# Dense products bank by bank, and neighbourhood scores with 128 rows throughout

## The chip, the cores and the metric

One core of one Trainium2 chip runs the whole program. The metric is the device time of one launch in microseconds (us), and lower is better. Five engines work side by side and wait for one another through semaphores: the matrix engine (PE in the profile, with its weight loads shown apart as PEld), the vector engine (DVE), the scalar engine (ACT), GpSimd (POOL) and the engine that issues most DMA transfers (SP). Matmuls read their operands from on-chip memory (SBUF) and write sums into eight banks of another memory (PSUM); a bank holds 512 columns of float32.

## What is computed

Two layers of a trunk over 512 latent tokens on a grid of 8 rows by 64 columns, and 256 context tokens ahead of them, 1024 channels wide. Each layer normalises and modulates the tokens, projects them once into four token mixers, weighs each mixer's output by a sigmoid gate, projects the sum, adds it to the residual, and ends with a squared-ReLU MLP:

```python
h = modulate(x, norm1, shift, scale)                # RMSNorm, adaLN
A, B, C, D = pool_mix, latent attention, neighbourhood attention, recurrence (all from h @ w_in)
proj = einsum('blnw,nwd->blnd', stack(A, B, C, D), w_br)
x += gate * (sum(sigmoid(gate_cols) * proj) @ w_o)
x += gate2 * (square(relu(modulate(x, norm2, ...) @ w1)) @ w2)
```

Context tokens read context tokens alone. In the neighbourhood attention a latent query reads the keys of an 8 x 16 window of the grid, with a bias by relative position, and all context keys; a context query reads the context keys. There are 4 heads of 64 channels. The second layer makes no output for the context tokens, so queries, gates and the MLP have 768 tokens in the first layer and 512 in the second; keys, values and forget gates have 768 in both.

## The kernel before

**Two parts of every operand.** Operands of the large products are split into a high part, rounded to the type float32r, and a low part, the rest. A product is three matmuls: high x high, high weight x low input, low weight x high input. All sum into the same bank.

**Dense products.** Channels stand on partitions, tokens along the columns. A unit of weights is 128 input rows x 8 k-tiles x 128 outputs (1024 input channels), loaded by SP, copied into its high part by the scalar engine (`unit`, line 69) and subtracted to its low part by the vector engine (line 70), one unit ahead of its use. `dense` (line 106) runs over the k-tiles; for each it calls `dense_step` (line 84), which goes through its targets. A target is a stretch of up to 512 tokens in one bank: 768 tokens have two targets, of 512 and 256 columns. `dense_step` issues the first two matmuls of each target (lines 88 and 89) and then, again for each target, the third (line 91). The room is a tile of two banks where the phase is "wide" (first layer, `p_big`, two such tiles) and a one-bank tile for each target otherwise. `dense_pair` runs two units together, one part of the tokens before the next; `dense_part` runs one part of the tokens alone. Both have their own loops.

**The merge.** `merge_steps` (line 1000) is a generator: for each output tile it makes a gate product of 8 k-tiles with a loop of its own, and yields after every second k-tile; then comes the product of the branch's output (2 k-tiles) and the sum. While a mixer runs, it calls `fill(n)`, which advances the generator of an earlier branch by n pieces. So pieces of gate products stand between the small matmuls of a mixer whose next operands come from other engines.

**Neighbourhood attention.** `na_att` runs over steps: a window of 128 queries (16 grid columns) and a head, 16 per layer, and in the first layer 128 context queries and a head, 8 in all. A step's scores are made by `products` (line 846). The keys of a head stand in 128 rows, the high part in the 64 rows where the head's channels are, the low part in the other 64. The query's high part `nqh` is copied into both halves (lines 853, 854), so that one 128-row matmul gives high query x both parts of the key (line 857). The query's low part `nql` fills only the head's 64 rows (line 855), and a second matmul of those 64 rows adds low query x high key (line 858). A window has two outputs of 256 columns in one bank, its local keys and the context keys, so four matmuls in turn; a context step has one output, so two. The softmax follows on the vector and scalar engines (lines 867 to 874), then transposes (line 705) and products with the values (line 890). Scores are one step ahead of their transposes.

**What sets the order.** The program is written in the order of the loops, and a planner arranges each engine's instructions from it ahead of the run, by priority and by when operands come free. On the chip each engine works through its list in that fixed order.

Of the kernel before, what the change touches and what calls it, by code (L numbers as in the profile page):

```python
# [8 lines left out]
F32 = mybir.dt.float32  # L9
# [26 lines left out]
# columns of the per-layer vectors  # L36
# [3 lines left out]
# channel-major units of the input projection  # L40
U_Z, U_G, U_Q, U_P, U_QA, U_CKV, U_NQ, U_NK, U_GATE = 0, 4, 6, 8, 10, 12, 13, 15, 17
# token-major groups
# [8 lines left out]
class K:  # L51
# [3 lines left out]
    # ---------------------------------------------------------------- weights  # L55
# [18 lines left out]
    def queue(self, specs):  # L74
        """Units are loaded and split a few ahead of the products that use them."""
        self.specs.extend(specs)
# [6 lines left out]
    # ---------------------------------------------------------------- dense products  # L83
    def dense_step(self, targets, w, kt, rhs, start, stop):
        """out += w[:, kt]^T @ rhs[:, kt, t0:t0+n], for each target (t0, n, out)."""
        mm = self.nc.tensor.matmul
        for t0, n, out in targets:
            mm(out, w.hi[:, kt], rhs.hi[:, kt, t0:t0 + n], start=start, stop=False)  # L88
            mm(out, w.hi[:, kt], rhs.lo[:, kt, t0:t0 + n], start=False, stop=False)  # L89
        for t0, n, out in targets:  # L90
            self.last_mm = mm(out, w.lo[:, kt], rhs.hi[:, kt, t0:t0 + n], start=False, stop=stop).ins  # L91

    def outputs(self, n):
        """Room for the products of the first n tokens: the targets of matmuls, and pieces (t0, n, ap) to read."""
        if self.wide:
            out = self.p_big.tile([P, 1024], F32, name="big")
            return [(a, min(n, a + 512) - a, out[:, a:min(n, a + 512)]) for a in range(0, n, 512)], [(0, n, out[:, :n])]
        return self.narrow_outputs(n)
# [7 lines left out]
    def dense(self, w, kts, rhs, n, narrow=False):  # L106
        targets, pieces = self.narrow_outputs(n) if narrow else self.outputs(n)
        for kt in range(kts):
            self.dense_step(targets, w, kt, rhs, kt == 0, kt == kts - 1)
        return pieces  # L110

    def dense_part(self, w, kts, rhs, t0, n, big):
        """The product for the tokens t0..t0+n alone."""
# [8 lines left out]
    def dense_pair(self, ws, kts, rhs, n, parts, between=None):  # L122
        """Two units at once, a part of the tokens (t0, n) before the next; between() is called early in the first."""
# [11 lines left out]
    def tokmajor(self, out, units, rhs, toks):  # L135
        """out[tokens, ncols] = rhs[:, :, tokens]^T @ w, w in units of some k-tiles each."""
# [17 lines left out]
    def lnexp(self):  # L154
        """Ln and Exp from one table set, for what follows on the engine"""
        self.tc.keep_in_program_order(self.nc.scalar.preload_act_table_set("natural_log_exp_and_others"))

    def rstd(self, out, ms, scale=1.0):
        """(ms * scale + eps) ** -0.5"""
# [3 lines left out]
    def rstd_rows(self, out, sqs, ones, n, hl, scale=1.0):  # L163
        """out[:, :n] = (scale * sum over partitions of sq + eps) ** -0.5 on every partition; the two parts of sq go to hl"""
# [13 lines left out]
    # ---------------------------------------------------------------- constants  # L178
# [8 lines left out]
    def late_constants(self, p):  # L187
        """What the first products do not need"""
# [39 lines left out]
    # ---------------------------------------------------------------- adaLN  # L228
    def silu(self, out, c, p, n):
        """c * sigmoid(c), for n values per partition"""  # L230
# [16 lines left out]
    def ada_first(self, quarter, raws, s32, p):  # L247
        """Shift and scale of the first norm for a quarter of the channels, for both streams."""
# [13 lines left out]
        # row 32 (2 m + j) + v: modulation m, stream v, the sum over even or odd channel tiles  # L262
# [10 lines left out]
    def ada_begin(self, p, l, ms, ahead=False):  # L273
        """The modulations ms of layer l, to be made one channel tile at a time: silu of both conditioning
        vectors along the free axis of every partition, and the list of what is left to do."""
# [23 lines left out]
    def ada(self, l, m, d):  # L299
        """mods[l][:, m*8+d, v] with channels on partitions, from rows of the transposed weights."""  # L300
# [19 lines left out]
    # ---------------------------------------------------------------- norm + modulation  # L320
    def stats(self, k, x, acc, n):
        """acc += x^2 over the channel tiles, k = 0..7"""
# [7 lines left out]
    def stats_end(self, acc, n, out, after=None, lnexp=True):  # L330
        """1 / rms for every token, on every partition; the sum over partitions queues behind a given product."""
# [9 lines left out]
    def modulate(self, k, x, rs, a, sh, h, groups):  # L341
        """h[:, k] = x * rs * a + sh in two parts"""
# [16 lines left out]
    # ---------------------------------------------------------------- D: HGRN2  # L359
    def hg_proj(self, l, u, h, nq, p, p2, p1):  # L360
        """Heads 2u, 2u+1: k, the cumulated log forget gates, q; forward on partitions 0-63, backward on 64-127."""
        nc = self.nc
        for hd in (2 * u, 2 * u + 1):
# [5 lines left out]
            # L = ln(1 + exp(-|z|)); sigmoid(-z) = exp(-(max(z,0)+L)); sigmoid(z) = exp(min(z,0)-L)  # L369
# [34 lines left out]
    def hg_values(self, h, p):  # L404
        """Values, and the rotary part of the latent attention's keys, with tokens on partitions"""
# [9 lines left out]
    def hg_state(self, hd, p):  # L415
        """Decayed states before each tile of 128 tokens, in both directions."""
# [9 lines left out]
        for g in range(3):  # L426
# [14 lines left out]
            # what a tile adds goes where the state after it belongs  # L441
# [15 lines left out]
    def hg_out(self, hd, S, grans, o, p, p2):  # L457
# [4 lines left out]
        for g in grans:  # L462
# [47 lines left out]
            # both tiles at once, in the two halves of the columns  # L510
# [47 lines left out]
    # ---------------------------------------------------------------- B: latent attention  # L558
    def rope(self, x, t, eng):
        """Rotates rows 64-95 of the latent tokens; rows 96-127 hold the other half of every pair."""  # L560
# [5 lines left out]
    def mla_pre(self, l, h, nq, y, po, p, p1):  # L566
        """Queries and keys per head, channels on partitions; values with tokens on partitions."""
# [11 lines left out]
        # the rotary part of the keys, on partitions 64-127  # L579
        kr = p.tile([P, T], F32, name="kr")  # L580
        # in the room of the branch's result, which comes later
# [14 lines left out]
        # their squares in two parts, one above the other  # L596
# [3 lines left out]
        # latent queries  # L600
# [14 lines left out]
        # latent keys and values  # L615
# [8 lines left out]
        # queries per head; their norms scale the scores  # L624
# [27 lines left out]
        # keys, two heads at once  # L652
# [26 lines left out]
    def softmax_pv(self, parts, pk, scale, minus, p):  # L679
        """Probabilities of 128 queries from scores in pieces, which scale (and minus, its negative) multiplies"""  # L680
# [17 lines left out]
    def transpose_p(self, pk, nk, dst):  # L698
        """dst[:, kt, :] = pk[:, kt*128:(kt+1)*128]^T"""
# [12 lines left out]
    def mla_att(self, l, nq, y, p, p2, p1):  # L712
        """Scores and probabilities of 128 queries of a head are one step ahead of their transposes and products."""
# [58 lines left out]
    # ---------------------------------------------------------------- C: neighbourhood attention  # L772
    def na_pre(self, l, h, nq, y, p, p1):
        nc, vec = self.nc, self.vec[l]
        self.nqT = p.tile([P, 2, T], F32, name="nqT")
        # both parts of a head's keys, one above the other; the higher part is where the head's channels are
# [5 lines left out]
        # columns of the grid first: token 64 r + c goes to 8 c + r  # L782
# [16 lines left out]
        # a unit's norm is made during the products of the next one  # L799
# [33 lines left out]
    def na_bias(self, l, p):  # L833
        """Bias and mask for the next two heads"""
# [6 lines left out]
    def na_att(self, l, nq, y, p, pb):  # L841
        """As in mla_att, one step ahead: scores of a window of queries and a head, then of the context."""
        nc = self.nc
        self.na_bias(l, pb)

        def products(outs, u, j, q0):
            """Scores of 128 queries from q0 of head 2 u + j: q * k, with k in both parts, and the lower part of q"""
# [4 lines left out]
            lo = p.tile([P, P], F32R, name="nql")  # L852
# [3 lines left out]
            for out, k0 in outs:  # L856
                nc.tensor.matmul(out, hi, k[:, k0:k0 + 256], start=True, stop=False)
                nc.tensor.matmul(out, lo[r], k[r, k0:k0 + 256], start=False, stop=True)  # L858
# [25 lines left out]
        def values(f, u, i, vt, pts):  # L884
# [7 lines left out]
            if f is window:  # L892
                # back to rows of the grid first
# [36 lines left out]
    # ---------------------------------------------------------------- A: pooling  # L930
    def pool(self, l, pss, nq, y, p):
# [5 lines left out]
        for u in range(2):  # L937
# [15 lines left out]
            while w < hi_w:  # L953
                s = w // 2
                for t0, n, o in segs:
                    # windows t-w .. t+w-1 from windows half as wide
# [22 lines left out]
    # ---------------------------------------------------------------- gates and merge  # L979
# [12 lines left out]
    def fill(self, n=1):  # L992
        """The next pieces of the products that fill the tensor engine's waits"""
# [3 lines left out]
    def merge_steps(self, l, n, half, h, y, nq, first):  # L997
        """ms[d] += sigmoid(gate) * (y @ w_branch), for four channel tiles d."""
# [3 lines left out]
        for i in range(5):  # L1002
            cur = None
            if i < 4:
# [3 lines left out]
                for kt in range(NK):  # L1008
                    self.dense_step(targets, w, kt, h, kt == 0, kt == NK - 1)
                    if kt % 2 and kt < NK - 1:  # L1010
# [4 lines left out]
                # sigmoid(x) = (1 + tanh(x / 2)) / 2; the half is taken where the sum of the branches is split  # L1015
# [16 lines left out]
    # ---------------------------------------------------------------- layer  # L1032
# [5 lines left out]
    def layer(self, l):  # L1038
# [18 lines left out]
        # ---- norm 1; the second layer's is made at the end of the first  # L1057
        if l == 0:
            es_h, h = self.open_h(R("h"))
            with L("n1") as p, L("n1t", 4) as self.p_tmp, L("ada0") as pa:  # L1060
# [7 lines left out]
                # three units at once, as the modulations come in  # L1068
# [28 lines left out]
                # the context tokens are a quarter behind the latent ones  # L1097
# [22 lines left out]
        # ---- mixers; each branch is merged while the next one runs  # L1120
# [55 lines left out]
        # ---- output projection, residual, norm 2  # L1176
# [7 lines left out]
        with L("n2") as p, L("n2t", 3) as self.p_tmp:  # L1184
# [3 lines left out]
            def resid(d, ps, groups, gate, stats=True):  # L1188
                """x += gate * ps, for the pieces (t0, n, v, po) of the tokens"""
# [13 lines left out]
            def by_parts(product, ds, gate, parts, early, store=None):  # L1203
                """The last products take one part of the tokens after the other, and the first part's norm is
                made during the second's products."""
# [41 lines left out]
            # ---- squared-ReLU MLP  # L1247
            with L("ff", 2) as p_f, L("fft", 2) as p_ft:
# [38 lines left out]
                if not last:  # L1287
                    es_wx, p_wx = opened(L("wx2", 2))
                    # the next layer's first norm, and its first products, which need the latent tokens alone
# [55 lines left out]
    def psum(self, wide):  # L1345
        """Two banks per product for 768 tokens, or one for 512"""
# [171 lines left out]
```

## Time and profile before

| | us |
|---|---|
| time before, median of 3 runs | 2334.12 |
| lowest and highest of the runs | 2333.78, 2336.18 |
| profiled execution, first to last instruction (its span) | 2332.4 |
| median of the runs less the span | 1.7 |
| matrix engine busy | 2275.7 (98%) |
| weight loads busy | 1886.6 (81%) |
| vector engine busy | 1484.6 (64%) |
| scalar engine busy | 941.4 (40%) |
| GpSimd busy | 174.5 (7%) |

The span is the profiled execution's only own time that the profile gives. The granted clock of the matrix engine over the span is 0.993. A matmul's duration in the trace overlaps with the next one's, so a sum of durations is not the time that they took: how closely matmuls follow one another is read from their starts in the timeline. In the timeline a row begins with the start, then the time; consecutive instructions of the same line are merged into one row (x2, x16).

### The profile page before, as it was taken

How to read it: one execution, taken by the hardware profiler on the slowest of the kernel's cores; microseconds unless marked ns; L12 is line 12 of the kernel's file. 1: busy time of each engine (PE TensorE's matmuls, PEld its weight loads, DVE VectorE, ACT ScalarE, POOL GpSimd, SP SyncE). 2: the span in 40 equal slices, each digit the busy share in tenths (PEclk: the TensorE clock that was granted, in tenths of full speed). 3: DMA queues.
4: the chain of work that ended last, by engine and by line, in shares of the span. 5: the costliest groups of instructions: out<-in, count | busy, mean ns of one | idle time of the engine just before them, and what ended most of it. 6: DMA issues, size and time to landing. Idle time of an engine off the chain costs nothing.

```text
span 2332.4 us, 32091 instructions
## 1 busy us (share of the span) xinstructions
PE 2275.7 (98%) x12642; PEld 1886.6 (81%) x12642; DVE 1484.6 (64%) x2754; ACT 941.4 (40%) x1664; POOL 174.5 (7%) x198
## 2 busy tenths in 40 slices
PE   6999999999999999999999999999999999999999
PEld 4877777888788888888888888776778788888887
DVE  6887857678874567655555578787865536544444
ACT  5545445446531342222222245464646524423221
POOL 0010100121111100000000000110011120000000
PEclk9999999999999999999999999999999999999999
DMA  7211110124333413333333222111112124233332
GB/s 272 78 37 46 37 61 19 46 105 160 114 138 116 145 37 126 117 113 116 117 117 127 99 87 80 55 55 61 46 68 93 55 91 135 91 97 93 99 99 82
DMA packets 64983, 217.58 MB, mean 93 GB/s; under 512 B 7937, under 2 KB 9857, under 8 KB 64577
## 3 DMA queue, kind: packets, MB, share of 16 engines
q1 hardware_dynamic: 63232, 210.16, 26.8%
q0 software_dynamic: 1024, 2.88, 0.4%
q10 hardware_dynamic: 576, 2.49, 0.3%
q8 instruction: 99, 1.62, 0.3%
q14 instruction: 52, 0.42, 0.1%
HBM read 210.27 MB, written 5.24 MB: 92 GB/s over the span
## 4 chain that ended last, share of the span: by engine, by line
PE 87%; DVE 8%; ACT 2%; issue 1%; DMA 1%; SPq 0%; ACTq 0%; DVEq 0%
PE big L88 24%; PE big L91 23%; PE big L89 23%; PE sm L705 2%; PE sm L738 2%; PE sm L501 1%; DVE wlo L70 1%; DVE hgc L387 1%; PE sm L750 1%; PE sm L517 1%; PE sm L858 1%; PE sm L88 1%; PE sm L89 1%; PE sm L91 1%; PE sm L890 1%
## 5 line engine op out<-in xcount | busy, mean ns | idle before, releaser
L88 PE MATMUL big<-hhi,whi 128*128 128x512 f32 (+1 forms) x1928 | 696.6, 362 | 9.7 <-DVE hgq L395 4.0
L89 PE MATMUL big<-hlo,whi 128*128 128x512 f32 (+1 forms) x1928 | 663.0, 357 | 1.0 <-DVE hlo L356 0.9
L69 ACT CAST whi<-raw 128x1024 fp32r<-128x1024 f32 (+1 forms) x268 | 279.2, 1045 | 862.5 <-PE big L89 801.4
L91 PE MATMUL big<-hhi,wlo 128*128 128x512 f32 (+1 forms) x1928 | 593.6, 358 | 1.1 <-DVE wlo L70 1.1
L70 DVE TENSOR_TENSOR wlo<-raw,whi 128x1024 fp32r<-128x1024 f32 (+1 forms) x268 | 328.2, 1228 | 377.2 <-ACT whi L69 373.0
L88 PEld LDWEIGHTS big<-hhi,whi 128*128 128x128 f32 x1928 | 364.2, 189 | 96.0 <-issue 9.1
L89 PEld LDWEIGHTS big<-hlo,whi 128*128 128x128 f32 x1928 | 365.1, 189 | 56.0 <-issue 3.3
L91 PEld LDWEIGHTS big<-hhi,wlo 128*128 128x128 f32 x1928 | 324.8, 190 | 29.1 <-issue 2.9
L88 PE MATMUL big<-fhi,whi 128*128 128x512 f32 x744 | 266.2, 358 | 0.0
L1192 DVE SCALAR_TENSOR_TENSOR xr<-big,mods,xr 128x256 f32<-128x256 f32 (+1 forms) x205 | 133.5, 663 | 200.7 <-PE big L91 200.5
L89 PE MATMUL big<-flo,whi 128*128 128x512 f32 x744 | 254.8, 356 | 0.0
L91 PE MATMUL big<-fhi,wlo 128*128 128x512 f32 x744 | 228.0, 357 | 0.0
L88 PEld LDWEIGHTS big<-fhi,whi 128*128 128x128 f32 x744 | 139.7, 188 | 31.9
L89 PEld LDWEIGHTS big<-flo,whi 128*128 128x128 f32 x744 | 139.7, 188 | 21.0
L1029 POOL TENSOR_TENSOR m<-m,gg 128x768 f32<-128x768 f32 (+1 forms) x48 | 88.6, 1850 | 600.5 <-DVE gg L1027 440.5
L91 PEld LDWEIGHTS big<-fhi,wlo 128*128 128x128 f32 x744 | 124.3, 189 | 10.8
L309 DVE CUSTOM_DVE_ANT_0 adaj<-raw,crow 128x1024 bf16<-128x1024 f32 x64 | 84.2, 1315 | 13.5 <-DMA raw<-in_ada_b_w_dram 12.7
L309 DVE CUSTOM_DVE_ANT_0 adaj<-adar,crow 128x1024 bf16<-128x1024 f32 x64 | 77.9, 1218 | 0.4
L88 PE MATMUL big<-yhi,whi 128*128 128x512 f32 x192 | 70.6, 368 | 0.0
L89 PE MATMUL big<-ylo,whi 128*128 128x512 f32 x192 | 66.6, 360 | 0.0
L479 POOL TENSOR_TENSOR hKL<-hgk,hE 64x128 f32<-64x128 f32 x80 | 39.4, 493 | 340.1 <-ACT hE L152 321.6
L152 ACT ACTIVATE mpk<-sm,sxm,krt 128x512 f32<-128x512 f32 (+1 forms) x72 | 46.9, 656 | 38.8 <-DVE sxm L687 38.7
(310 smaller groups left out, 3367.2 us busy)
## 6 DMA issues: line engine op xcount, KB each, us to landing
raw<-in_w_ff_dram SPq DMA_DIRECT2D x128, 512.0 KB, 3.5
raw<-in_w_cm_dram SPq DMA_DIRECT2D x98, 512.0 KB, 3.2
adar<-in_ada_b_w_dram SPq DMA_DIRECT2D x48, 512.0 KB, 3.3
raw<-in_ada_b_w_dram SPq DMA_DIRECT2D x32, 512.0 KB, 3.3
adaw<-in_ada_a_dram SPq DMA_DIRECT2D x16, 512.0 KB, 7.7
raw<-in_w_br_dram SPq DMA_DIRECT2D x16, 512.0 KB, 3.4
raw<-in_w_out_dram SPq DMA_DIRECT2D x16, 512.0 KB, 3.5
nbias<-in_nab_dram SPq DMA_DIRECT2D x8, 384.0 KB, 3.9
```

Source lines behind the costliest of these rows:

```text
L69: nc.scalar.copy(hi[:, :n], raw[:, :n])
L70: nc.vector.tensor_tensor(lo[:, :n], raw[:, :n], hi[:, :n].bitcast(F32), ALU.subtract)
L88: mm(out, w.hi[:, kt], rhs.hi[:, kt, t0:t0 + n], start=start, stop=False)
L89: mm(out, w.hi[:, kt], rhs.lo[:, kt, t0:t0 + n], start=False, stop=False)
L91: self.last_mm = mm(out, w.lo[:, kt], rhs.hi[:, kt, t0:t0 + n], start=False, stop=stop).ins
L152: self.nc.scalar.activation(out, in_, f, **kw)
L309: nc.vector.tensor_tensor_reduce(junk, w, self.srow[:, v], 1.0, 0.0, ALU.mult, ALU.add, x[:, v:v + 1])
L479: (nc.vector if n >= 2 else nc.gpsimd).tensor_tensor(v(KL[lo_:hi_, n])[:, :, h0:h0 + H], v(ks)[lo_:hi_, :, h0:h0 + H], v(E[lo_:hi_, n])[:, ...
L705: nc.tensor.transpose(pt[:, (kt - a) * P:(kt - a + 1) * P], pk[:, kt * P:(kt + 1) * P], self.ident)
L738: nc.tensor.matmul(ps[:, 0:b - a], qx[:, qr], kx[:, a:b], start=i == 0, stop=i == 2)
L1029: nc.gpsimd.tensor_tensor(m, m, g, ALU.add)
L1192: self.last_v = nc.vector.scalar_tensor_tensor(x, ps[:, po:po + n], self.mods[l][:, gate + d, v:v + 1], x, ALU.mult, ALU.add).ins
```

## The change

Three places change, and comments are taken out (which moves line numbers by a few).

`dense` and `merge_steps` go through all k-tiles of one target before the next target, and so fill one bank after the other. In `merge_steps` the yields go by columns done, a quarter of the product at a time, where they went by k-tiles. With one target (512 tokens in the second layer) the order is the same as before.

In `na_att` the low part of the queries gets four tiles of its own of 128 rows, two for each place of the head in its pair, used in turn. The 64 rows of other channels are set to zero once per layer on GpSimd, and the second matmul takes all 128 rows of the tile and of the keys.

```diff
     def dense(self, w, kts, rhs, n, narrow=False):
         targets, pieces = self.narrow_outputs(n) if narrow else self.outputs(n)
-        for kt in range(kts):
-            self.dense_step(targets, w, kt, rhs, kt == 0, kt == kts - 1)
+        for t, kt in self.steps_of(targets, kts):
+            self.dense_step([t], w, kt, rhs, kt == 0, kt == kts - 1)
         return pieces
 
+    def steps_of(self, targets, kts):
+
+        return [(t, kt) for t in targets for kt in range(kts)]
...
         self.na_bias(l, pb)
 
+        los = [[pb.tile([P, P], F32R, name=f"nql{j}{i}") for i in range(2)] for j in range(2)]
+        turn = [0, 0]
+        for j in range(2):
+            for t in los[j]:
+                nc.gpsimd.memset(t[64 - 64 * j:128 - 64 * j].bitcast(F32), 0.0)
...
             hi = p.tile([P, P], F32R, name="nqh")
-            lo = p.tile([P, P], F32R, name="nql")
+            lo = los[j][turn[j] % 2]
+            turn[j] += 1
             nc.scalar.copy(hi[r], q)
             nc.scalar.copy(hi[o], q)
             self.tt(lo[r], q, hi[r].bitcast(F32), ALU.subtract)
             for out, k0 in outs:
                 nc.tensor.matmul(out, hi, k[:, k0:k0 + 256], start=True, stop=False)
-                nc.tensor.matmul(out, lo[r], k[r, k0:k0 + 256], start=False, stop=True)
+                nc.tensor.matmul(out, lo, k[:, k0:k0 + 256], start=False, stop=True)
...
                 targets, ((_, _, pg),) = self.outputs(nq)
-                for kt in range(NK):
-                    self.dense_step(targets, w, kt, h, kt == 0, kt == NK - 1)
-                    if kt % 2 and kt < NK - 1:
+                done, quarter = 0, NK * nq // 4
+                for t, kt in self.steps_of(targets, NK):
+                    self.dense_step([t], w, kt, h, kt == 0, kt == NK - 1)
+                    done += t[1]
+                    if done >= quarter and (t, kt) != (targets[-1], NK - 1):
+                        done -= quarter
                         yield
```

## Rows read from the trace of the kernel before

**Rows 1.** The page: busy time of the matrix engine, and the chain by engine.
```profile
PE 2275.7 (98%) x12642; PEld 1886.6 (81%) x12642; DVE 1484.6 (64%) x2754; ACT 941.4 (40%) x1664; POOL 174.5 (7%) x198
...
PE 87%; DVE 8%; ACT 2%; issue 1%; DMA 1%; SPq 0%; ACTq 0%; DVEq 0%
```

**Rows 2.** Busy time of PE, PEld, DVE, ACT, POOL in both neighbourhood stages.
```profile
553.00:668.00 115.00, 113.26 (x698) 90.45 (x696) 95.01 (x243) 61.25 (x169) 17.64 (x9) 1.00 0.37 129
...
1781.00:1860.00 79.00, 79.00 (x452) 59.40 (x451) 46.49 (x148) 49.15 (x137) 12.48 (x8) 1.00 0.21 71
```

**Rows 3.** Timeline of PE: one k-tile of 768 tokens, and the 24th after it.
```profile
1180.20 0.40 PE L88 MATMUL big<-fhi,whi 128*128 128x512 f32 x1
1180.44 0.40 PE L89 MATMUL big<-flo,whi 128*128 128x512 f32 x1
1180.68 0.28 PE L88 MATMUL big<-fhi,whi 128*128 128x256 f32 x1
1180.80 0.28 PE L89 MATMUL big<-flo,whi 128*128 128x256 f32 x1
1180.92 0.51 PE L91 MATMUL big<-fhi,wlo 128*128 128x512 f32 x2
...
1205.48 0.40 PE L88 MATMUL big<-fhi,whi 128*128 128x512 f32 x1
```

**Rows 4.** Timeline of PE: ends of a run of 512, and of 256 columns.
```profile
816.35 0.40 PE L88 MATMUL big<-mhi,whi 128*128 128x512 f32 x1
...
831.78 0.39 PE L91 MATMUL big<-mhi,wlo 128*128 128x512 f32 x1
...
835.97 0.28 PE L91 MATMUL sm<-mhi,wlo 128*128 128x256 f32 x1
...
841.37 0.28 PE L91 MATMUL sm<-mhi,wlo 128*128 128x256 f32 x1
```

**Rows 5.** Timeline of PE: the first scores, a window's four, a context step.
```profile
553.63 0.28 PE L857 MATMUL sm<-nkT,nqh 128*128 128x256 f32 x1
...
556.36 0.40 PE L89 MATMUL big<-hlo,whi 128*128 128x512 f32 x1
...
576.07 0.36 PE L857 MATMUL sm<-nkT,nqh 128*128 128x256 f32 x1
576.37 0.38 PE L858 MATMUL sm<-nkT,nql 64*128 64x256 f32 x1
...
577.30 0.50 PE L88 MATMUL big<-hhi,whi 128*128 128x512 f32 x1
577.63 0.40 PE L89 MATMUL big<-hlo,whi 128*128 128x512 f32 x1
...
602.68 0.36 PE L857 MATMUL sm<-nkT,nqh 128*128 128x256 f32 x1
...
603.62 0.40 PE L89 MATMUL big<-ylo,whi 128*128 128x512 f32 x1
```

**Rows 6.** Timeline of PE: scores of latent attention, 96 rows.
```profile
495.61 0.37 PE L738 MATMUL sm<-mk1hi,mqhi 96*128 96x256 f32 x1
495.81 0.29 PE L738 MATMUL sm<-mk1lo,mqhi 96*128 96x256 f32 x1
...
496.05 0.39 PE L88 MATMUL big<-hhi,whi 128*128 128x512 f32 x1
496.28 0.39 PE L89 MATMUL big<-hlo,whi 128*128 128x512 f32 x1
```

**Rows 7.** Groups of DVE, 553 to 668 us: busy, mean ns, idle before, releasers.
```profile
L309 DVE CUSTOM_DVE_ANT_0 adaj<-raw,crow 128x1024 bf16<-128x1024 f32 x30 | 39.8, 1326 | 3.7 <-DMA raw<-in_ada_b_w_dram 3.6
L70 DVE TENSOR_TENSOR wlo<-raw,whi 128x1024 fp32r<-128x1024 f32 x10 | 12.5, 1251 | 5.1 <-ACT whi L69 5.0
```

**Rows 8.** Groups of DVE, 65 to 320 us: weight splits of the recurrence stage.
```profile
L70 DVE TENSOR_TENSOR wlo<-raw,whi 128x1024 fp32r<-128x1024 f32 (+2 forms) x20 | 23.7, 1189 | 12.4 <-ACT whi L69 12.3
```

**Rows 9.** Timeline of POOL: the bias scaling as the first scores begin.
```profile
556.49 5.45 POOL L838 TENSOR_SCALAR nbias<-nbias 128x768 f32<-128x768 f32 x2 [2.31 <-DMA nbias<-in_nab_dram]
```

## The prediction

> **What bounds the kernel now.** I read the page first: the matrix engine is busy 98% of the span, and the chain that ended last is 87% matmuls, 8% vector engine, 2% scalar engine [rows 1]. Busy time counts the overlapping part of pipelined matmuls, so it does not say how fast they follow one another. For that I read the timeline of the matrix engine and take the distance from one start to the next. The sums by stretch come next: in the two neighbourhood stages the matrix engine is busy 113.26 of 115 us (layer 0) and 79.00 of 79 us (layer 1), at a granted clock of 1.00, while the vector engine has 95.01 and 46.49 us of work [rows 2]. So nearly everywhere the end is set by how densely matmuls are issued, and the question is what the two edits do to the distance between starts. One place is close to another limit: the vector engine in layer 0's neighbourhood stage.
>
> **Part 1, dense products bank by bank.** No matmul is added or removed; six per k-tile stay six, each with its weight load. Before, a k-tile of 768 tokens goes 512, 512, 256, 256, 512, 256 columns (the last two print as one row). From 1180.20 to 1205.48 us lie 24 k-tiles, so one takes 25.28 / 24 = 1.0533 us [rows 3]. The new order is already in the trace, in the output projection's last units, which take one part of the tokens at a time: 512 columns in a row start 15.43 us / 68 = 0.2269 us apart (816.35 to 831.78), and 256 columns in a row 5.40 / 45 = 0.1200 us apart (835.97 to 841.37) [rows 4]. A k-tile in the new order is then 3 x 0.2269 + 3 x 0.1200 = 1.0407 us, 12.6 ns less.
>
> How many k-tiles change order, from the loops (only calls of `dense` and `merge_steps` with 768 columns; `dense_pair` and `dense_part` stay): layer 0 has 7 recurrence units, 3 for latent attention, 4 for neighbourhood, 32 gates, 3 output units and 30 of the first MLP matrix, 79 units of 8 = 632; 32 branch products of 2 = 64; 58 second-matrix products of 4 = 232; together 928. Layer 1 has 768 columns only for keys and forget gates, 4 + 1 + 2 units of 8 = 56. 984 x 12.6 ns = 12.4 us. Some 168 of them lie in the recurrence stages, where matmuls wait for others now and then; I leave out half of their 2.1 us: 11.4 us.
>
> The change of order also moves needs. The low part of a weight is needed two matmuls after its unit begins (0.45 us), not four (0.72, 1180.20 to 1180.92), so 0.27 us earlier. The last k-tile of the input is needed earlier too, but inputs are complete there. The pieces of `fill` keep their size in columns (3 steps of 512, 3 of 512, 2 and 2, then 6 of 256), so a wait is filled by as much as before. A wide product is still read after its last matmul. I price all of this at nothing; if the low part of a weight were late each time, 0.27 us x 86 units = 23 us would be the bound on the bad side, and a few units starting earlier the bound on the good side.
>
> [...]
>
> **Part 2, the low part of the queries on 128 rows.** Each group of scores alternates 128-row and 64-row matmuls in one bank. The timeline shows what that costs: a window's four (576.07, .37, .67, .99) are about 0.31 us apart, and the dense 512-column matmul behind them needs 0.33 us before the next one starts; from 576.07 to 577.63 it is 1.56 us [rows 5]. The nearest row without a change of rows to 64 is in latent attention: 96-row matmuls of 256 columns behind the same transposes, also accumulating in one bank: 0.20 us after the first, then 0.12, and 0.23 for the dense matmul behind them [rows 6]. Four 128-row matmuls and that one dense one then take 0.20 + 3 x 0.12 + 0.23 = 0.79 us, 0.77 less. A context step (two matmuls) goes from 0.94 (602.68 to 603.62) to 0.20 + 0.12 + 0.23 = 0.55, 0.39 less. Each layer's first two windows stand together, eight matmuls and no transposes ahead: 2.73 us (553.63 to 556.36) against 8 x 0.12 + 0.23 = 1.19, 1.54 less [rows 5]. There are 16 windows per layer and 8 context steps in layer 0: 28 x 0.77 + 8 x 0.39 + 2 x 1.54 = 27.8 us, 15.4 in layer 0 and 12.3 in layer 1. A few groups have transposes or value products behind them, where less is saved; I take 15 and 12. That 128 rows cost nothing over 64 is the one thing not shown; the bounds are zero extra (96 rows against 128 in rows 4 and 6, both 0.12) and all 27 us (if the 0.31 came from something else).
>
> What of it reaches the end. Layer 1: 79 - 12 = 67 us, the vector engine's work is 46.49 and the scalar engine's 49.15 [rows 2]; I keep 11. Layer 0: 115 - 15 = 100 us, against 95.01 us of vector work, of which 39.8 are adaLN sums (30 of 1326 ns), plus 5.0 us that it waits for the scalar engine's weight copies [rows 2, 7]. That is an engine without slack, in a strict order; what is late next is probabilities and weight splits. I take 4 us lost, 11 kept; the bounds are 0 and 15 lost.
>
> Four fills with zeros per layer are new on GpSimd, about as large as the smallest tiles it handles, under 1 us together. Where they stand matters more: the scaling of the bias for the next two heads is issued ahead of them and in layer 0 runs from 556.49 to 561.94 [rows 9], while the first scores begin at 553.63 [rows 5]. If the zeros stood behind it, the first group would be 8 us late, with gate products ready to go in between; queued behind it on GpSimd are only the merges' additions. I take 1 us for both layers; the bounds are 0 and 16. The four low tiles, two per head parity, are reused every fourth step, not every second; that costs nothing.
>
> **Sum.** 11.4 + 11 + 11 - 1 = 32.4 us. The profiled span is 2332.4 us, so 2300.0; the median of the runs shown, 2334.12, is 1.7 above the span, so 2301.7. I predict 2302.
>
> **Rivals.**
> A. *Order makes no difference in the wide tile*: what I measured for 512 in a row is a stretch of one part of the tokens, and the wide product could still run at 1.053 per k-tile. Against it: the weights, inputs and banks are of the same kind. For it: the rows of the new order come from one stage only. The dense term is zero: 2302 + 11 = 2313. [...]
> B. *The vector engine takes over in layer 0's neighbourhood stage*: 95.01 us of work plus its waits fill the stage, and none of the 11 us come through. 2313.
> C. *The 0.31 us is not from the 64 rows* but from two operands in turn in one bank. Against it stand the 96-row groups at 0.12 in the same pattern [rows 6]. Part 2 gives nothing: 2302 + 22 - 1 = 2323.
> D. *Nothing is lost on the way*: all 12.4 and 27 us arrive, 2295, or a few lower where the order written anew happens to fit better.
> E. *Slower*: in the recurrence stages the weight splits move ahead. A unit's product ends sooner, its buffer comes free, and the next split enters the vector engine's queue ahead of the recurrence's own chain. A split is 1189 ns, with 20 of them in layer 0's stage [rows 8]; with as many in layer 1, 40 x 1.19 = 48 us if each delays the chain by its whole length. It decides from 28 of the 40, 32.4 / 1.19. Against it: a unit shrinks by only 0.1 us, far less than a split. 2302 + 48 = 2350.
>
> **How the numbers follow.** The forecast has 0.60, A 0.10, B 0.10, C 0.04, D 0.10, E 0.04; 0.02 are left for A, B and C together, about no change. A measurement of this kernel can tell 0.2%, about 4.7 us. Faster by more than that is the forecast with A to D: 0.94; within it 0.02; slower 0.04. The range from 2288 to 2320 holds the forecast, A, B and most of D, and leaves out C, E and the tails.
>
> **What would show it.** Start-to-start distances in the changed kernel: 0.227 us for 512 columns in a row and 0.12 for 256 within wide dense units, with 1.04 us per k-tile in the MLP (right), or 1.053 (A). Score groups at 0.12 us apart with full-length dense matmuls behind them at 0.23 (right), or still 0.31 (C). Layer 1's neighbourhood stage 11 us shorter and layer 0's about as much; if layer 0's stays at 110 or more with new waits of transposes for probabilities, it is B. The first low-part matmul waiting for a fill on GpSimd would show that the zeros stand wrong. Longer waits for the vector engine in the recurrence stages would be E. A total above 2320 would mean that a term of the sum is missing, one below 2288 that I left out a gain.

## The result, and the profile after

The changed kernel took 2313.63 us (median of 4 runs, 2311.43 to 2315.95) beside 2334.28 us for the kernel before on the same chip: a ratio of 0.9913, 95% interval 0.9899 to 0.9927, so 20.6 us faster. Forecast were 2302 us and a range of 2288 to 2320. The direction and the range hold; 11.6 of the 32 us are missing.

The page of the changed kernel, busy time by engine and the chain of waits (before: [rows 1]):

```profile
PE 2246.3 (97%) x12642; PEld 1879.7 (81%) x12642; DVE 1484.4 (64%) x2754; ACT 939.0 (41%) x1664; POOL 172.5 (7%) x206
...
PE 81%; DVE 12%; ACT 3%; issue 2%; DMA 1%; POOL 0%; SPq 0%; ACTq 0%; DVEq 0%; POOLq 0%
```

TensorE (the matrix engine, PE) has as many instructions as before and is still busy nearly everywhere, but the chain's share on VectorE (DVE) has grown from 8% to 12%: a first hint that the vector engine now holds up more of it. The span is 2312.3 us, 20.0 less, near the runs' difference, so the profile can be read for the rest.

The timeline of TensorE in the changed kernel, in the MLP's second matrix (before: [rows 3]); the first row of four k-tiles of 512 columns, of four of 256, and of the unit that follows, then of the fourth unit after the first:

```profile
1167.80 0.40 PE L88 MATMUL big<-fhi,whi 128*128 128x512 f32 x1
...
1170.54 0.28 PE L88 MATMUL big<-fhi,whi 128*128 128x256 f32 x1
...
1171.98 0.40 PE L88 MATMUL big<-fhi,whi 128*128 128x512 f32 x1
...
1184.52 0.40 PE L88 MATMUL big<-fhi,whi 128*128 128x512 f32 x1
```

Twelve matmuls of 512 columns take 2.74 us, 0.2283 each, and twelve of 256 take 1.44, 0.1200 each. From 1167.80 to 1184.52 lie 16 k-tiles, 1.045 us each, where before it was 1.0533.

The same engine in the neighbourhood stage of layer 0: a context step's two scores with the dense matmul behind them, and a window's four (before: [rows 5]):

```profile
604.05 0.36 PE L868 MATMUL sm<-nkT,nqh 128*128 128x256 f32 x1
604.25 0.28 PE L869 MATMUL sm<-nkT,nql 128*128 128x256 f32 x1
604.37 0.39 PE L88 MATMUL big<-hhi,whi 128*128 128x512 f32 x1
604.60 0.40 PE L89 MATMUL big<-hlo,whi 128*128 128x512 f32 x1
...
607.33 0.36 PE L868 MATMUL sm<-nkT,nqh 128*128 128x256 f32 x1
607.53 0.28 PE L869 MATMUL sm<-nkT,nql 128*128 128x256 f32 x1
607.65 0.28 PE L868 MATMUL sm<-nkT,nqh 128*128 128x256 f32 x1
607.77 0.28 PE L869 MATMUL sm<-nkT,nql 128*128 128x256 f32 x1
607.88 0.40 PE L88 MATMUL big<-hhi,whi 128*128 128x512 f32 x1
608.12 0.40 PE L89 MATMUL big<-hlo,whi 128*128 128x512 f32 x1
```

The starts are 0.20, 0.12, 0.12, 0.11 us apart, and 0.24 for the dense matmul: 0.79 us from 607.33 to 608.12, as forecast to the hundredth. The context step takes 0.55.

Then what was not forecast. First GpSimd as layer 0's first scores begin, with the fills (L854) and the bias scaling (L842; before: [rows 9]), then TensorE there:

```profile
552.50 0.34 POOL L854 MEMSET nql<- 64x128 f32 x2
554.90 2.13 POOL L842 TENSOR_SCALAR nbias<-nbias 128x768 f32<-128x768 f32 x1 [2.06 <-DMA nbias<-in_nab_dram]
557.09 0.34 POOL L854 MEMSET nql<- 64x128 f32 x2
```

```profile
553.45 0.40 PE L89 MATMUL big<-hlo,whi 128*128 128x512 f32 x1
557.34 0.58 PE L869 MATMUL sm<-nkT,nql 128*128 128x256 f32 x1 [3.50 <-POOL nql L854]
...
558.57 0.63 PE L88 MATMUL big<-hhi,whi 128*128 128x512 f32 x1
559.00 0.63 PE L89 MATMUL big<-hlo,whi 128*128 128x512 f32 x1
...
562.41 0.39 PE L88 MATMUL big<-hhi,whi 128*128 128x512 f32 x1
562.64 0.40 PE L89 MATMUL big<-hlo,whi 128*128 128x512 f32 x1
```

Two fills come in time. The other two stand behind a bias scaling that waits 2.06 us for its table, and the second head's low matmul waits for them at the head of TensorE's list, with the gate product queued behind it. After the wait, matmuls of 512 columns start 0.43 us apart, not 0.23, until 562.41. The stretches of the same kernel (length, busy time and count of PE, PEld, DVE, ACT, POOL, then granted clock, DMA share, GB/s) say why:

```profile
554.00:557.30 3.30, 0.00 (x0) 0.00 (x0) 3.30 (x4) 0.00 (x0) 2.35 (x3) 0.74 0.99 335
557.30:560.80 3.50, 3.46 (x10) 2.88 (x11) 3.50 (x10) 0.59 (x2) 2.53 (x2) 0.50 0.84 275
560.80:564.00 3.20, 3.20 (x12) 2.54 (x11) 2.80 (x10) 2.00 (x8) 0.00 (x0) 0.75 0.68 229
```

The granted clock falls to 0.50, the 1.2 GHz level, and comes back to 2.4 GHz within the third stretch. From 557.34 to 562.41 run three matmuls of 256 columns and ten of 512; they take 5.1 us, where at 0.12 and 0.23 us each they would take 2.7, so another 2.4 us are lost. Layer 1 has two waits of TensorE and then stretches with the lower clock:

```profile
1770.63 0.53 PE L869 MATMUL sm<-nkT,nql 128*128 128x256 f32 x1 [2.17 <-POOL nql L854]
1773.26 0.58 PE L869 MATMUL sm<-nkT,nql 128*128 128x256 f32 x1 [0.81 <-POOL nql L854]
```

```profile
1773.20:1776.60 3.40, 3.34 (x9) 2.79 (x10) 2.38 (x12) 2.19 (x9) 2.27 (x3) 0.50 0.81 258
1776.60:1780.00 3.40, 3.40 (x17) 2.74 (x15) 1.18 (x4) 0.40 (x2) 0.00 (x0) 0.86 0.01 2
```

GpSimd there shows that only the second of these waits comes from the bias scaling. The first pair of fills stands behind the transfers of the values (L834 and the one after it), which GpSimd issues once the reordered values have landed (`vperm`, 4.45 us of waiting):

```profile
1768.80 0.78 POOL L834 DMA_DIRECT2D nv<-vperm  x1 [4.45 <-DMA vperm<-nvt]
...
1770.38 0.34 POOL L854 MEMSET nql<- 64x128 f32 x2
1770.82 2.13 POOL L842 TENSOR_SCALAR nbias<-nbias 128x768 f32<-128x768 f32 x1
1773.01 0.34 POOL L854 MEMSET nql<- 64x128 f32 x2
```

Both neighbourhood stages of the changed kernel as stretches, beside [rows 2]:

```profile
553.00:668.00 115.00, 108.24 (x732) 92.06 (x731) 100.79 (x253) 59.50 (x172) 17.97 (x10) 0.97 0.38 129
...
1781.00:1860.00 79.00, 77.90 (x474) 62.73 (x474) 46.57 (x136) 45.52 (x122) 12.18 (x8) 1.00 0.20 62
```

In layer 0 TensorE idles 6.8 us in 115, where it was 1.7, and VectorE has 100.79 us of work in the stretch, up from 95.01.

For the experiments I measure a stage from its first score matmul to the first matmul of the output projection (`big<-mhi,whi`). Before, layer 0's is 553.63 to 770.78, 217.2 us; changed, 551.94 to 761.53, 209.6. Layer 1's is 146.4 us before (1783.98 to 1930.33) and 142.7 changed (1767.60 to 1910.32).

### The profile page after: what moved, and what is told of

Same layout as the page of the kernel before. It is cut to its first block, busy times and chain, and to the rows that moved or that the text cites. A ratio compares the mean times of both kernels' runs of the same rounds, so it can differ in the third digit from the quotient of the medians.

```text
span 2312.3 us, 32101 instructions
## 1 busy us (share of the span) xinstructions
PE 2246.3 (97%) x12642; PEld 1879.7 (81%) x12642; DVE 1484.4 (64%) x2754; ACT 939.0 (41%) x1664; POOL 172.5 (7%) x206
## 4 chain that ended last, share of the span: by engine, by line
PE 81%; DVE 12%; ACT 3%; issue 2%; DMA 1%; POOL 0%; SPq 0%; ACTq 0%; DVEq 0%; POOLq 0%
PE big L91 22%; PE big L89 22%; PE big L88 22%; DVE wlo L70 2%; PE sm L742 2%; PE sm L709 1%; PE sm L505 1%; DVE hgc L391 1%; PE sm L754 1%; PE sm L521 1%; DVE adaj L313 1%; PE sm L88 1%; PE sm L89 1%; PE sm L91 1%; DVE hKL L483 1%
## 5 line engine op out<-in xcount | busy, mean ns | idle before, releaser
L91 PE MATMUL big<-hhi,wlo 128*128 128x512 f32 (+1 forms) x1928 | 690.1, 358 | 1.3 <-DVE wlo L70 1.3
L89 PE MATMUL big<-hlo,whi 128*128 128x512 f32 (+1 forms) x1928 | 689.2, 358 | 1.3 <-DVE hlo L360 1.2
L91 PEld LDWEIGHTS big<-hhi,wlo 128*128 128x128 f32 x1928 | 367.5, 191 | 55.2 <-issue 3.8
L89 PE MATMUL big<-flo,whi 128*128 128x512 f32 (+1 forms) x744 | 265.5, 357 | 0.0
L88 PE MATMUL big<-fhi,whi 128*128 128x512 f32 (+1 forms) x744 | 265.3, 357 | 0.0
L91 PE MATMUL big<-fhi,wlo 128*128 128x512 f32 (+1 forms) x744 | 264.8, 356 | 0.0
L91 PEld LDWEIGHTS big<-fhi,wlo 128*128 128x128 f32 x744 | 140.4, 189 | 20.3
L313 DVE CUSTOM_DVE_ANT_0 adaj<-raw,crow 128x1024 bf16<-128x1024 f32 x64 | 81.7, 1277 | 15.2 <-DMA raw<-in_ada_b_w_dram 14.2
L91 PE MATMUL big<-yhi,wlo 128*128 128x512 f32 x192 | 69.0, 359 | 0.0
```

Of the source, the lines that this page charges most:

```text
L313: nc.vector.tensor_tensor_reduce(junk, w, self.srow[:, v], 1.0, 0.0, ALU.mult, ALU.add, x[:, v:v + 1])
```

## Experiments

Each was timed in five rounds beside the kernel before on the same chip (its median 2333.6 to 2334.1 us in all of them). There are two theories: the zeros and the lower clock behind them ate the rest, or VectorE in layer 0 did.

**The bank order alone.** The kernel before with only `dense` and `merge_steps` changed.

```diff
-        for kt in range(kts):
-            self.dense_step(targets, w, kt, rhs, kt == 0, kt == kts - 1)
+        for t, kt in self.steps_of(targets, kts):
+            self.dense_step([t], w, kt, rhs, kt == 0, kt == kts - 1)
```

> The kernel before with the order bank by bank alone (dense and merge_steps), scores as before. By the theory that a wide k-tile went from 1.059 to 1.048 us in the MLP of the changed kernel, 928 k-tiles give 9 to 10 us: 2324 to 2326, ratio 0.996, wherever it stands. By rival A (order makes no difference) 2334, ratio 1.000. If the order also moves work of the other engines into each other's way, it is above 2334.

Measured: 2323.87 us, ratio 0.9955 (0.9942 to 0.9967), 9.9 us less. Over 984 k-tiles that is 10.1 ns each. Layer 0's neighbourhood stage is 216.2 us here (550.27 to 766.48), 0.9 less than before; layer 1's is 147.0, no shorter.

**The scores alone.** The changed kernel with the old order of `dense` and `merge_steps` (the diff above, reversed).

> The changed kernel with the old order of the dense products, so the 128-row low part alone. By the theory that the spacing saves 27 us and that late zeros and the half clock behind them take 12 back, it is 10 to 13 us below before: 2321 to 2324, ratio 0.995, with a wait for the zeros of 2 to 4 us in each layer. If the zeros are late only because the dense order moved the first scores, the waits are not here and it is near 2310.

Measured: 2322.59 us, ratio 0.9945 (0.9932 to 0.9957), 11.2 us less, with waits for the zeros in this kernel too:

```profile
558.79 0.58 PE L865 MATMUL sm<-nkT,nql 128*128 128x256 f32 x1 [4.32 <-POOL nql L850]
...
1781.17 0.39 PE L865 MATMUL sm<-nkT,nql 128*128 128x256 f32 x1 [2.18 <-POOL nql L850]
1783.80 0.58 PE L865 MATMUL sm<-nkT,nql 128*128 128x256 f32 x1 [1.13 <-POOL nql L850]
```

The two parts add up within what these runs can tell: 9.9 + 11.2 = 21.1, against 20.6 for both. So little or nothing is lost between them; it is mainly the scores' part that is short, 11.2 instead of 21.

**The zeros earlier.** The low tiles get a pool that is opened earlier, and their fills stand ahead of the bias.

```diff
+        with self.tc.high_priority(1500):
+            for j in range(2):
+                for t in los[j]:
+                    nc.gpsimd.memset(t[64 - 64 * j:128 - 64 * j].bitcast(F32), 0.0)
+        self.na_bias(l, pb)
...
-            with L("nas", 2) as p1, L("nab") as pb:
+            with L("nab") as pb, L("nas", 2) as p1:
```

> The changed kernel with the four low tiles first in their pool, that pool ahead of the step's other tiles, and the zero fills at a higher priority, so that they stand ahead of the loads of the values on GpSimd. By the theory of the zeros the waits of 3.5, 2.2 and 0.8 us and the half clock behind them go, some 12 us: 2300 to 2303 us. By the rival that the vector engine limits layer 0's neighbourhood stage, new waits for probabilities take layer 0's share, 6 us: 2307 to 2309.

Measured: 2305.91 us, ratio 0.9876 (0.9862 to 0.9889), 27.9 us less than before and 7 less than the changed kernel. No wait for zeros is left. Layer 1's stage is 137.0 us, 5.7 shorter than in the changed kernel: its two waits, 2.98 us, and 2.7 that are left for the clock. Layer 0's gains only 2.3, since another wait comes there. TensorE, the clock behind its wait (a stretch), and VectorE in this kernel:

```profile
563.36 0.63 PE L709 MATMUL sm<-c_ident,npk 128*128 128x128 f32 x4 [3.27 <-DVE npk L885]
```

```profile
563.30:567.60 4.30, 4.25 (x24) 4.28 (x25) 3.42 (x12) 2.83 (x9) 0.00 (x0) 0.60 0.37 126
```

```profile
555.25 1.23 DVE L313 CUSTOM_DVE_ANT_0 adaj<-raw,crow 128x1024 bf16<-128x1024 f32 x1 [2.78 <-DMA raw<-in_ada_b_w_dram]
...
561.18 1.23 DVE L313 CUSTOM_DVE_ANT_0 adaj<-raw,crow 128x1024 bf16<-128x1024 f32 x1
...
562.72 0.88 DVE L885 TENSOR_SCALAR npk<-npk,nz 128x512 f32<-128x512 f32 x2
```

VectorE works through its list in order. One adaLN sum (it makes a part of the modulations from one row of weights) waits 2.78 us for that row, another stands right ahead of the first probabilities (`npk`), and TensorE's transposes wait 3.27 us for those, with the clock at 0.60 afterwards. Before, TensorE and VectorE show the same place so:

```profile
563.41 0.63 PE L705 MATMUL sm<-c_ident,npk 128*128 128x128 f32 x4 [1.64 <-DVE npk L874]
```

```profile
562.78 0.88 DVE L874 TENSOR_SCALAR npk<-npk,nz 128x512 f32<-128x512 f32 x2
```

VectorE is no later than before: it begins these probabilities at 562.72 us, where it was 562.78. TensorE is there 1.7 us sooner, about what its first two windows of scores save (1.54 in the forecast), and waits 1.6 us longer. After the shorter wait the granted clock stayed at 1.00.

**The sums of the neighbourhood stage moved to the merge behind it.** As the last, without these lines of `na_att`:

```diff
-            if n % 4 == 1:
-                self.ada_some(1)
```

> As the one with early zeros, and the six adaLN steps of layer 0's neighbourhood steps (12 sums of 1.3 us on the vector engine) fall to the merge after it, which has slack. If the vector engine limits layer 0's stage, this is 4 to 8 us below the one with early zeros, and transposes no longer wait for probabilities there. If it doesn't, the two are within 2 us.

Measured: 2314.66 us, ratio 0.9915 (0.9902 to 0.9929), 8.8 us slower than with the early zeros: a miss for both theories. A sum that was issued earlier still stands ahead of the probabilities, now with 4.51 us of waiting, and in the merge a sum that waits 3.30 us for its row stands ahead of the product of a branch with its gate (`gg`), and TensorE waits with it:

```profile
564.95 1.09 PE L709 MATMUL sm<-c_ident,npk 128*128 128x128 f32 x4 [4.77 <-DVE npk L885]
...
725.05 0.80 PE L88 MATMUL big<-hhi,whi 128*128 128x512 f32 x1 [4.99 <-DVE gg L1039]
```

**No sums in layer 0.** The early zeros, and layer 0's modulations 2 to 5 as constants.

```diff
             self.ada_begin(p_a, 0, range(2, 6))
+            self.ada_left = []
+            nc.vector.memset(self.mods[0][:, 16:48], 0.5)
+            nc.vector.memset(self.a2[0], 1.0)
```

> The kernel with the zeros ahead of the bias tables, and in addition layer 0's modulations 2 to 5 left out: they are constants, so that neither their sums on VectorE nor the loads of their rows are in layer 0's neighbourhood stage and the merge behind it. This part of the computation is missing. Theory 1 (in layer 0 the sums, or the loads that they wait for, stand ahead of the first probabilities on VectorE and hold up TensorE, wait 3.56 us with the lower clock behind it, and cost single waits later): 6 to 8 us below the kernel with the early zeros, so 2298 to 2300 us, and no wait of the transposes at about 563 us. Theory 2 (layer 0's stage is held by VectorE's own work on the scores, which stays): within 2 us of 2306, and the wait at about 563 us stays. The loads' share of the DMA engines goes too, so by itself this run does not tell sums from loads.

Measured: 2296.63 us, ratio 0.9844 (0.9829 to 0.9858), 9.3 us below the early zeros. Layer 0's stage runs from 551.64 to 750.56, 198.9 us, and TensorE is busy 114.66 of 115 us at full clock, with VectorE at 69.01:

```profile
553.00:668.00 115.00, 114.66 (x795) 98.75 (x795) 69.01 (x196) 64.75 (x180) 17.78 (x9) 1.00 0.19 61
```

So once the sums and their loads are away, TensorE has next to no wait left in this stretch.

**The sums without their row loads.** The early zeros, and layer 0's sums read a resident row:

```diff
+        if l == 0:
+            return self.srow[:, d % 2]
```

> The kernel with the zeros ahead of the bias tables, and in addition layer 0's sums of modulations 2 to 5 read a resident row instead of one that is loaded for each: the sums stay as many and as long, their row loads are gone, and these modulations hold other values. Theory 1a (it is the load of a row that the sum waits for, 2.78 us at 555.25, that makes the first probabilities late): 5 to 7 us below the kernel with the early zeros, so 2299 to 2301 us, near the run without sums. Theory 1b (it is the time of the sums on VectorE, 30 of 1.33 us): within 2 us of 2306, and only the run without sums gains. The half of both would be about 2302.

Measured: 2309.47 us, ratio 0.9894 (0.9878 to 0.9911), 3.6 us above the early zeros. Without loads to pace them, the sums gather in front: VectorE has 112.51 us of work in the same stretch (101.28 with the early zeros), and new waits come, for the low part of the queries and for probabilities:

```profile
555.00 0.36 PE L871 MATMUL sm<-nkT,nql 128*128 128x256 f32 x1 [0.57 <-DVE nql L153]
...
556.97 0.36 PE L871 MATMUL sm<-nkT,nql 128*128 128x256 f32 x1 [1.26 <-DVE nql L153]
```

The loads alone are then not the cause. How much of the 9.3 us is vector time and how much rows that come late, this run does not split, since the order of the sums changed with it.

**The first sums later.** The early zeros, with `n % 4 == 1 and n > 1` in `na_att` and the merge's first sum left for later.

> The kernel with the zeros ahead of the bias tables, and the first sum steps of layer 0's neighbourhood stage left for later, so that no sum and no wait for a row stands ahead of the first probabilities; all sums are still made, the two left out at the front come at the end of the sums in the stages behind. Theory 1 (the place of the sum ahead of the first probabilities is what costs): the wait of 3.56 us at about 563 us is gone and with it the lower clock behind it, 2 to 5 us below the kernel with the early zeros, so 2301 to 2304 us. Theory 2 (wherever a sum stands it waits for its row, and the wait moves to the next probabilities or into the merge, as when the sums of a whole stage were moved): 2306 to 2310 us.

Measured: 2312.92 us, ratio 0.9915 (0.9900 to 0.9929), 7 us slower. The first wait shrinks to 2.02 us, and a later sum that waits 3.44 us for its row stops the merge:

```profile
562.60 0.63 PE L709 MATMUL sm<-c_ident,npk 128*128 128x128 f32 x4 [2.02 <-DVE npk L885]
...
721.71 0.79 PE L88 MATMUL big<-hhi,whi 128*128 128x512 f32 x1 [4.56 <-DVE gg L1041]
```

**The softmax planned first.** The early zeros, and the body of `window` and the softmax of `context` under a higher priority.

```diff
+            with self.tc.high_priority(1500):
                 nc.vector.tensor_tensor_reduce(sb, ps[:, 0:256], ...
```

> The kernel with the zeros ahead of the bias tables, and in addition the softmax of the neighbourhood scores is planned ahead of the other work of the vector and scalar engines, so that the probabilities of a step stand ahead of sums in VectorE's queue where both are ready; nothing is left out and all sums stay in their stage. Theory 1 (the place of the sums in the queue is what costs): the waits for probabilities in layer 0, 3.56 us at 563 and some 2 us in single waits, mostly go, 3 to 6 us below the kernel with the early zeros, so 2300 to 2303 us. Theory 2 (VectorE's total work in layer 0's stage is too much, wherever the sums stand): within 2 us of 2306; another product is late in place of the probabilities.

Measured: 2305.58 us, ratio 0.9876 (0.9862 to 0.9890), no difference. Single waits later on are fewer, but the first stays, 3.40 us at 562.84: the sum at 556.24, which waits 2.82 us for its row, is ahead of the scores' softmax itself.

**The kernel before without sums.** The lines of the run without sums, in the kernel before.

> The kernel before, with layer 0's modulations 2 to 5 left out (constants in their place), so without their sums and row loads; this part of the computation is missing. Leaving the same out of the changed kernel with early zeros gave 9.3 us. If VectorE's sums held up layer 0 before as well, this run gains as much, 2323 to 2326 us, and the loss is no effect of the change. If the longer scores hid the sums, it gains only its waits of 1.6 us and a little, 2329 to 2333 us, and the change has uncovered VectorE there.

Measured: 2331.26 us, ratio 0.9988 (0.9979 to 0.9997), 2.4 us less. The same lines give 9.3 us in the kernel with the new scores, the bank order and the early zeros. So before the change most of the sums were hidden, and the change uncovered them. With the sums left out of both kernels, layer 0's stage goes from 215.0 us (552.79 to 767.80) to 198.9, 16.1 less, of which the bank order alone gave 0.9: 15.2 us for the scores, where 15 were forecast.

**That one sum behind the probabilities.** The softmax first, and the last sum issued ahead of the scores (`if t in (1, 3)`, not `if t % 2`, in `na_pre`) made later.

> The kernel with early zeros and the softmax planned first, and in addition the one sum of layer 0 that stood ahead of the first scores' softmax in VectorE's queue (1.23 us at 556.24, behind an idle time of 2.82 us for its row) is made later; nothing is left out. If that one sum and its wait cause TensorE's wait of 3.40 us at 562.84 and the lower clock behind it: the first probabilities are ready some 4 us earlier, the wait falls below 0.5 us, and the time is 3 to 5 us below the kernel with early zeros and softmax first, so 2300 to 2303 us. If the wait moves to a later sum or into the merge, as twice before: 2305 to 2309 us.

Measured: 2304.39 us, ratio 0.9877 (0.9861 to 0.9894). The first transposes now wait 0.53 us, at 558.17. The wait has moved to the next sum; TensorE and VectorE in this kernel:

```profile
564.72 0.70 PE L709 MATMUL sm<-c_ident,npk 128*128 128x128 f32 x4 [3.83 <-DVE nm L881]
```

```profile
562.13 1.23 DVE L313 CUSTOM_DVE_ANT_0 adaj<-raw,crow 128x1024 bf16<-128x1024 f32 x1 [3.79 <-DMA raw<-in_ada_b_w_dram]
```

The kernels with early zeros, softmax first and this sum later are 2304 to 2306 us and can't be told apart. They are the fastest that compute everything: their intervals, 0.9861 to 0.9894, lie below the changed kernel's, 0.9899 to 0.9927.

## Why the prediction was right and wrong

**The dense term was right in kind and a little large.** Forecast 11.4 us, measured 9.9 in the run of the bank order alone. The step that failed is 12.6 ns per k-tile: I took 0.2269 us for 512 columns from a long run of them, and a wide unit goes back and forth between the banks. Its first matmuls of 512 start 0.23 to 0.24 us apart (0.2283 in the mean of twelve), so a unit of four k-tiles gains 8.3 ns each, not 12.6; why the first ones are slower stays open. The count of 984 was a little high too: in layer 1 the planner had already put part of the 768-column units in bank order (in the kernel before, the unit at 1406.37 us runs all its 512 columns first), and some 27 of the 56 k-tiles there alternate. Rival A, no difference, is refuted by the same rows and by the run. The Trainium skill, "TensorE: Matmul & The Clock Gate", section "Back-to-back issue gap", has columns / 2.4 plus 2.5 ns as the gap of an isolated matmul, an estimate of 0.216 and 0.109 us for 512 and 256 columns, and about 0.131 us for 512 columns in a stream. The changed kernel's rows agree with neither: in a stream they show 0.228 and 0.120.

**Moved needs at nothing: right.** In the changed kernel TensorE's dense products wait 1.3 us in two places for the low part of a weight, before 1.1 in two. Rival E did not come about.

**The scores' spacing was right.** 0.79 us per window, 0.55 per context step; rival C is refuted, and the rows show no cost of 128 rows over 64. With the zeros early, layer 1's stage gives 9.3 us of the 11 that I kept (12.3 as counted from groups); without sums before and after, layer 0's stage gives the 15 that I counted. The Trainium skill, "TensorEngine Tiling (Array Packing)", section "Key Properties", says that a change of the tiling mode drains TensorE. The rows agree with that: score matmuls that alternated 128 and 64 rows were 0.31 us apart [rows 5], and all on 128 rows they are 0.12. No run here tells such a drain from another cost of the 64-row matmuls. The page names no price for it; here the alternation cost 0.77 us for a window's four.

**The zeros were the step most mis-sized.** I named the bias scaling ahead of the fills, bounded it at 16 us and took 1. The waits are 3.50, 2.17 and 0.81 us, 6.5 in all. The place was right for the first and the last; the 2.17 us in layer 1 come from the transfers of the values, which I had not seen ahead of the fills (I wrote that only the merges' additions queue there). The reason for a low value was wrong: gate products are ready, but they stand behind the waiting matmul in TensorE's list, so they fill nothing. And I did not price the clock. The Trainium skill, "TensorE: Matmul & The Clock Gate", section "What's actually happening", says that the engine drops from 2.4 to 1.2 GHz after idle time. The trace agrees: the granted clock was 0.50 after the waits of 3.50 and 2.17 us. From the rows, 2.4 us went that way in layer 0, and 2.7 are left for it in layer 1. Moving the zeros gave 7.3 us back, of the 11.6 that waits and clock come to, because layer 0 ran into its next limit.

**That limit is the term of 4 us lost in layer 0.** The mechanism, VectorE without slack in a strict order, was right, and rival B in part. The size was not: the runs without sums show 9.3 us under the new scores against 2.4 under the old, so with the zeros out of the way 7 us of what the change gives are lost to the sums and their loads there, and I had 4. I compared sums of busy time (95.01 us and 5.0 of waiting in a stage of 100). What decides is single places: a sum at the head of VectorE's queue that waits 2.8 to 4.5 us for its row, with probabilities or a gate behind it, and a lower clock afterwards. Where the sum stands is not the whole of it: four ways to move the sums or what they stand before moved the wait too; two cost 7 and 9 us, two gave nothing that these runs can tell.

The missing 11.6 us by terms: 1.5 for the dense products; 6.3 for the zeros with the clock (7.3 measured, 1 forecast); 2.0 in layer 0, whose stage gives 9.9 us with early zeros (553.50 to 760.80), 0.9 of them the bank order's, so 9.0 of the 11 forecast for the scores; 1.7 in layer 1. That is 11.5. So close a fit is in part luck: the stretch ahead of the first product in the new order (59.20 us before), which no edit touches, was 1.4 us shorter in the changed kernel's profiled execution, and terms of this size are at the edge of what these runs can tell.

## What to carry to other kernels

On an engine that is busy 98% of the time, price a new wait at its length and, where it is a few us long, at what a lower clock behind it costs (after 1.64 us in the kernel before there was none, after 2.17 us here there was), and ask what stands behind the waiting instruction in its own list, not what would be ready. When work is taken from the bounding engine in a stage, look at single instructions of the next engine that wait for a transfer, not at its sum of busy time. An initial value that is written once belongs ahead of everything that waits on the same queue.

## What was not expected of the hardware

A wait of 3.5 us was followed by 5.1 us at the lower clock. In layer 1 the matmuls ran at the lower clock from the end of the first wait, of 2.17 us, for 6.8 us, with the second wait of 0.81 us among them. The clock cost 2.4 us beside waits of 3.5, and 2.7 beside 3.0, nearly as much as the waits themselves. The first matmuls of 512 columns after a run of 256 start 0.23 to 0.24 us apart where a long run has 0.227, while 256 columns are at 0.120 from the first on.
